# Cross-attention values in one 512-column product, and two heads' weighted sums moved behind half an output product

## The chip, the cores and the metric

The kernel runs on one core of a Trainium2 chip. The metric is the device time of one execution in microseconds; smaller is better. It is one launch that holds the whole decoder trunk of two layers, with every weight streamed from HBM once.

## The reference, cut to what matters

Each of the two layers has three token mixers that run side by side, a cross-attention into 256 memory tokens, and a SwiGLU FFN. The change touches the cross-attention and the last FFN product of the second layer.

```python
def cross_attention(h, mm, wq, wk, wv, wo):
    q = (h @ wq).reshape(B, S, XA_HEADS, XA_HEAD_DIM)     # S = 256 tokens, 4 heads of 256
    k = (mm @ wk).reshape(B, M, XA_HEADS, XA_HEAD_DIM)    # M = 256 memory tokens
    v = (mm @ wv).reshape(B, M, XA_HEADS, XA_HEAD_DIM)
    s = jnp.einsum('bshd,bmhd->bhsm', q, k).astype(jnp.float32) * (XA_HEAD_DIM ** -0.5)
    p = jax.nn.softmax(s, axis=-1).astype(v.dtype)
    o = jnp.einsum('bhsm,bmhd->bshd', p, v).reshape(B, S, D_MODEL)   # D_MODEL = 1024
    return o @ wo
...
x = x + (jax.nn.silu(h @ w1[l]) * (h @ w3[l])) @ w2[l]    # D_FF = 2816
```

## The kernel before, in words

**Split products.** Every float32 matrix is kept as two parts, `hi` (rounded to the format fp32r that TensorE takes) and `lo` (what is left), and a product is hi·hi + hi·lo + lo·hi. So a weight tile is made ready in three steps. `fetch` (lines 93 to 110) asks for a tile `raw` of 128 x 1024 by a DMA from SP's queue (line 102), ScalarE (ACT) rounds it into `hi` (line 106), and VectorE (DVE) subtracts to get `lo` (line 107, recorded as line 67, the helper `tt`). There are 5 buffers of `raw` and 4 each of `hi` and `lo`. Tile n therefore takes the `hi` and `lo` buffers of tile n-4, and its rounding waits until TensorE has read the last of tile n-4. `weights(cols)` hands out the next columns of this one stream, so the order of the stream in HBM is the order of the matmuls. `plan` (lines 79 to 87) says from which columns each tile is filled; the first 8 tiles of a layer are gathered from two runs, in pieces of 512 columns.

**Orders.** TensorE's instructions run in the order in which the code issues them (`InOrder`, line 43 in every row of TensorE). On ACT, DVE, GpSimd (POOL) and SP a scheduler sets the order of the instructions when the program is built, and each engine then works through its list in that order, waiting where an operand or a buffer is not there yet.

**The stage around the change.** After queries and keys, the values are made by `chunk_N`: activations are stationary, and a weight row of `n` columns moves, three matmuls for each of 2 blocks of memory tokens and each of 8 steps k. `values` (lines 538 to 541) calls it three times: columns 0 to 511 as one product with n = 512, then 512 to 767 and 768 to 1023 as two products with n = 256. Each result lies in PSUM as `xv` and is evicted into the tile `vt`: ACT writes the hi part (line 540), DVE the lo part (line 541, recorded as line 67). Between the steps, hooks issue the scores (`s`), the transposes of the softmax (`pT`, `turned`) and the weighted sums (`av`, `weighted`). `weighted(h)` is 12 matmuls of 256 columns for head h. It reads `vt` in the order block 0 hi (2 matmuls), block 0 lo (1), block 1 hi (2), block 1 lo (1), for two halves of the head's columns. Its result is split into `ox` by ACT and DVE. Heads 0 and 1 lie in the columns 0 to 511 of `vt`, heads 2 and 3 in 512 to 1023.

The output product `xo` (`chunk_T`) comes in chunks of 256 output columns. The first two chunks are cut in half: their steps k = 0 to 3, which read heads 0 and 1 of `ox`, come first, and k = 4 to 7 later. Before, the order is weighted(2), half of chunk 0, weighted(3), half of chunk 1:

```python
for c in range(2):
    weighted(2 + c)
    xo[c] = chunk_T(of(ox), KT, f"xo{l}_{c}", ks=range(0, 4))
```

A half chunk is 16 matmuls and uses exactly one weight tile. In layer 1 the second half of the values takes tiles 82 to 85, the half of chunk 0 tile 86, and the half of chunk 1 tile 87.

**The end of the program.** The last FFN product has three chunks of 256 columns (`chunk_T`) and two of 128 (`chunk_y` with one block, names w2_6 and w2_7), 22 steps each. Then the final norm follows.

Of the kernel before, what the change touches and what calls it, by code (L numbers as in the profile page):

```python
# [11 lines left out]
F32 = mybir.dt.float32  # L12
F32R = mybir.dt.float32r
AF = mybir.ActivationFunctionType
ALU = mybir.AluOpType
AX = mybir.AxisListType

P = 128
D = 1024
S = 256  # L20
L = 2
KT = D // P
FF = 2816
FT = FF // P
EPS = 1e-6
TW = 1024
LAYER_COLS = 163840
NPAR = 48
WARM = 9
AHEAD = 1  # L30

IN = dict(ax=0, ac=256, ab=512, q=768, k=1024, v=1280, g=1792, z=2304, gates=2816)


# [20 lines left out]
def decoder_trunk(ctx: ExitStack, tc: tile.TileContext, a, out):  # L55
    nc = tc.nc
    V, A, G, T = nc.vector, nc.scalar, nc.gpsimd, InOrder(tc, nc.tensor)
# [6 lines left out]
    pss = ctx.enter_context(tc.tile_pool(name="pss", bufs=4, space=bass.MemoryType.PSUM))  # L64

    def tt(e, o, x, y, op):
        e.tensor_tensor(o, x, y, op=op)  # L67

    def f32(t):
        return t.bitcast(F32)  # L70
# [5 lines left out]
    ws = a["ws"]  # L76
    tiles = ws.shape[0]

    pair_of = [(c + 512 * k, 512) for k in range(KT) for c in (0, 512 * KT)]
    plan = pair_of + [(c, TW) for c in range(2 * 512 * KT, LAYER_COLS, TW)]  # L80
    plan = [(l * LAYER_COLS + c, n) for l in range(L) for c, n in plan]
    pieces = []
    for c, n in plan:
        if not pieces or pieces[-1][-1][0] + pieces[-1][-1][2] == TW:
            pieces.append([])
        at = sum(m for _, _, m in pieces[-1])
# [25 lines left out]
    def weights(cols):  # L112
        pos = state["pos"]
        while state["loaded"] <= min(pos // TW + AHEAD, tiles - 1):
            fetch()
        o = pos % TW
        state["pos"] = pos + cols
        hi, lo = ready[pos // TW]
        return hi[:, o:o + cols], lo[:, o:o + cols]


    def chunk_T(xs, kt, name, hooks=None, ps=None, ks=None):


        if ps is None:
            ps = psm.tile([P, 2, 2, S], F32, tag="mm", name=name)
        for k in ks or range(kt):
            if hooks and k in hooks:
                hooks[k]()
            wh, wl = weights(2 * P)  # L130
            x = xs(k)
            for i in range(2):
                c = slice(i * P, (i + 1) * P)
                T.matmul(ps[:, i].rearrange("p t s -> p (t s)"), wh[:, c], x.rearrange("p t s -> p (t s)"),
                         start=(k == 0), stop=False, skip_group_check=True)
                T.matmul(ps[:, i, 1], wl[:, c], x[:, 0], start=False, stop=(k == kt - 1), skip_group_check=True)
        return ps

    def chunk_N(xs, name, hooks=None, n=512):

        ps = psm.tile([P, 2, 512], F32, tag="mm", name=name)
        for k in range(KT):
            if hooks and k in hooks:
                hooks[k]()
            wh, wl = weights(n)
            x = xs(k)
            for b in range(2):
                sl = slice(b * P, (b + 1) * P)
                T.matmul(ps[:, b, 0:n], x[:, 0, sl], wh, start=(k == 0), stop=False)
                T.matmul(ps[:, b, 0:n], x[:, 1, sl], wh, start=False, stop=False)  # L150
                T.matmul(ps[:, b, 0:n], x[:, 0, sl], wl, start=False, stop=(k == KT - 1))
        return ps[:, :, 0:n]

    def chunk_pair(xs, names, hooks):

        pair = [psm.tile([P, 2, 512], F32, tag="mm", name=name) for name in names]
        for k in range(KT):
            if k in hooks:
                hooks[k]()
            x = xs(k)  # L160
            for ps in pair:
                wh, wl = weights(512)
                for b in range(2):
                    sl = slice(b * P, (b + 1) * P)
                    T.matmul(ps[:, b], x[:, 0, sl], wh, start=(k == 0), stop=False)
                    T.matmul(ps[:, b], x[:, 1, sl], wh, start=False, stop=False)
                    T.matmul(ps[:, b], x[:, 0, sl], wl, start=False, stop=(k == KT - 1))
        return pair

    def chunk_y(xs, kt, name, n=2):  # L170

        ps = pss.tile([P, 2, S], F32, tag="sm", name=name)
        for k in range(kt):
            wh, wl = weights(n * P)
            x = xs(k)
            for i in range(n):
                c = slice(i * P, (i + 1) * P)
                T.matmul(ps[:, i], wh[:, c], x[:, 0], start=(k == 0 and i == 0), stop=False, skip_group_check=True)
                T.matmul(ps[:, i], wh[:, c], x[:, 1], start=False, stop=False, skip_group_check=True)
                T.matmul(ps[:, i], wl[:, c], x[:, 0], start=False, stop=(k == kt - 1 and i == n - 1),  # L180
                         skip_group_check=True)
        return ps

    def of(t, k0=0):
        return lambda k: t[:, k0 + k]
# [19 lines left out]
    xT = res.tile([P, KT, S], F32, name="xT")  # L205
    xs = res.tile([P, KT, 2, S], F32R, name="xs")
# [99 lines left out]
    for l in range(L):  # L306
# [5 lines left out]
        def pair(x):  # L312
            return x.rearrange("p b (h d) -> p b h d", h=8)
# [15 lines left out]
        t, ra, rbb = pair(mb[:, 0:2]), pair(mb[:, 2:4]), pair(mb[:, 4:6])  # L329
# [47 lines left out]
        for h in range(4):  # L377
            ps = pss.tile([P, 512], F32, tag="sm", name=f"sc{l}_{h}")
# [12 lines left out]
        for g in range(4):  # L391
            sl = slice(g * 64, (g + 1) * 64)
# [20 lines left out]
        for b in range(2):  # L413
            ps = pss.tile([P, 512], F32, tag="sm", name=f"o{l}_{b}")
# [27 lines left out]
        for c in range(12):  # L442
            t = summed(chunk_T(of(xs), KT, f"gt{l}_{c}"))
# [10 lines left out]
            if c == 6:  # L454
                if l == 0:
                    rows_kept(rm_n, "rm", rm)
                mmt = wrk.tile([P, KT, 2, S], F32R, tag="M", name=f"mmt{l}", bufs=1)
# [7 lines left out]
            if c == 1:  # L465
                for i in range(2):
                    ps = transposes(rr.rearrange("p b h d -> p b (h d)"), 2 * i, f"rT{l}")
                    for j in range(2):
                        f = 2 * i + j
# [4 lines left out]
        for c in range(4):  # L474
            ev = []
            for br, (k0, kn) in enumerate(((0, 2), (2, 4), (6, 2))):
                ps = chunk_y(of(mo, k0), kn, f"y{l}_{c}_{br}")
# [32 lines left out]
        vt = wrk.tile([P, 2, 2, D], F32R, tag="B", name=f"vt{l}", bufs=1)  # L510
# [24 lines left out]
        def turned(h):  # L535
            split(pt[:, 2 * h:2 * h + 2], transposes(pps[h], 0, f"pT{l}_{h}"))

        def values(c, n, hooks):
            ps = chunk_N(of(mmt), f"xv{l}_{c}", hooks, n)
            A.activation(vt[:, :, 0, c:c + n], ps, AF.Copy)  # L540
            tt(V, vt[:, :, 1, c:c + n], ps, f32(vt[:, :, 0, c:c + n]), ALU.subtract)

        ox = wrk.tile([P, 8, 2, S], F32R, tag="op", name=f"ox{l}", bufs=2)

        def weighted(h):
            ps = pss.tile([P, 2, S], F32, tag="sm", name=f"av{l}_{h}")
            for d in range(2):
                ns = slice((2 * h + d) * P, (2 * h + d + 1) * P)
                for b in range(2):
                    m = 2 * h + b  # L550
                    T.matmul(ps[:, d], vt[:, b, 0, ns], pt[:, m, 0], start=(b == 0), stop=False)
                    T.matmul(ps[:, d], vt[:, b, 0, ns], pt[:, m, 1], start=False, stop=False)
                    T.matmul(ps[:, d], vt[:, b, 1, ns], pt[:, m, 0], start=False, stop=(b == 1))
            split(ox[:, 2 * h:2 * h + 2], ps)

        def at(**kw):
            fs = dict(s=scores, t=turned, w=weighted)
            return {int(k[1:]): (lambda f=fs[v[0]], h=int(v[1]): f(h)) for k, v in kw.items()}

        qhooks = [None, None, at(k4="s0"), at(k4="s1", k6="t0")]  # L560
        for j in range(4):
            split(qx[:, 2 * j:2 * j + 2], summed(chunk_T(of(xs), KT, f"q{l}_{j}", hooks=qhooks[j])))
        values(0, 512, at(k1="s2", k2="t1", k4="s3", k6="t2"))
        values(512, 256, at(k2="t3", k6="w0"))
        values(768, 256, at(k4="w1"))


        xo = [None, None]
        for c in range(2):
            weighted(2 + c)  # L570
            xo[c] = chunk_T(of(ox), KT, f"xo{l}_{c}", ks=range(0, 4))

        acc = new_acc(f"acc_ffn{l}")
        for j in range(4):
            if j < 2:
                ps = chunk_T(of(ox), KT, f"xo{l}_{j}", ps=xo[j], ks=range(4, KT))
            else:
                ps = chunk_T(of(ox), KT, f"xo{l}_{j}")
# [22 lines left out]
        hooks = {2: {0: ffn_cols}, 3: {0: ffn_rows}}  # L601
        ts = []
        part = [chunk_T(of(xs), KT, f"f{l}_{c}", ks=range(0, KT - 2)) for c in range(2)]
        for c in range(FT):
            if c < 2:
                ps = chunk_T(of(xs), KT, f"f{l}_{c}", ps=part[c], ks=range(KT - 2, KT))
            else:
                ps = chunk_T(of(xs), KT, f"f{l}_{c}", hooks=hooks.get(c))
# [18 lines left out]
    table = wrk.tile([P, 1], F32, tag="table", name="table", bufs=1)  # L627
    A.activation(table, acc[:, 0:1], AF.Sqrt)
    for n in (6, 7):
        ps = chunk_y(hidden, FT, f"w2_{n}", 1)  # L630
        tt(V, xT[:, n], ps[:, 0], xT[:, n], ALU.add)
        tt(V, lastsq[:, n - 6], xT[:, n], xT[:, n], ALU.mult)
        if n == 6:
            tt(G, acc, acc, lastsq[:, 0], ALU.add)
            for m in range(7):
                V.tensor_scalar_mul(xT[:, m], xT[:, m], gfin[:, m:m + 1])
# [33 lines left out]
def _stream(x, l):  # L670
    w = x["w_in"][l]
    c = lambda n, m: w[:, IN[n]:IN[n] + m]
    parts = [_rows(c(n, 512), 512) for n in ("q", "v", "z", "g")]
# [57 lines left out]
```

## Time and profile before

| what | value |
|---|---|
| median of 3 runs | 968.31 us (968.21, 968.31, 970.08) |
| profiled execution, its own time | 969.4 us |
| span of that execution, first to last instruction | 967.6 us |
| TensorE (PE) busy | 951.8 us, 98% of the span |
| VectorE (DVE) busy | 713.7 us, 74% |
| ScalarE (ACT) busy | 539.8 us, 56% |
| mean granted TensorE clock | 0.995 |

The span is what the profile's rows lie in; 1.8 us of the execution's own time lie around it. A row of a timeline gives the start and the length of an instruction (of a run of alike ones, with their count), and in brackets the idle time of its engine ahead of it and what ended that. The ends of matmuls are modelled, so the pace of TensorE is read from start to start. A granted clock of 1.00 is TensorE's upper level (2.4 GHz), 0.50 its lower one (1.2 GHz).

### The profile page before, as it was taken

What the parts mean: (1) busy time and instruction counts of PE and PEld (TensorE: products, weight loads), DVE (VectorE), ACT (ScalarE), POOL (GpSimd) and SP (SyncE); (2) the same over time, 40 slices, a digit from 0 to 9 for tenths busy, and PEclk for the clock granted to TensorE, in tenths of its full rate; (3) what the DMA queues carried; (4) which work ended last, traced back from release to release, by engine and by line L of the source; (5) the groups of instructions that cost most, each with busy time, mean ns of one, the idle gap of its engine ahead of it and who ended that gap; (6) DMA issues with size and microseconds to landing.
All of it is one profiled execution on the core that took longest, in us unless ns stands there. A gap on an engine that the chain in (4) does not pass through costs nothing.

```text
span 967.6 us, 14606 instructions
## 1 busy us (share of the span) xinstructions
PE 951.8 (98%) x5622; PEld 836.8 (86%) x5622; DVE 713.7 (74%) x884; ACT 539.8 (56%) x740; POOL 296.1 (31%) x232
## 2 busy tenths in 40 slices
PE   8999999999999999999999989999999999999996
PEld 6788889888998888888888878998889888888886
DVE  7679789886768866657655896799776778666654
ACT  6565765565645755654456465545665466656431
POOL 5943021320114644432134230024100345444211
PEclk9999999999999999999999999999999999999998
DMA  9664665555546565555656355555644556556541
GB/s 310 245 228 145 192 203 186 190 182 170 172 133 194 177 198 191 193 187 180 197 179 194 111 180 193 195 179 172 196 153 151 154 187 191 187 194 194 180 151 44
DMA packets 52630, 175.53 MB, mean 181 GB/s; under 512 B 6096, under 2 KB 6608, under 8 KB 52560
## 3 DMA queue, kind: packets, MB, share of 16 engines
q1 hardware_dynamic: 52128, 174.03, 55.9%
q8 instruction: 44, 0.72, 0.3%
q10 hardware_dynamic: 432, 0.57, 0.2%
q14 instruction: 26, 0.21, 0.1%
HBM read 173.53 MB, written 1.05 MB: 180 GB/s over the span
## 4 chain that ended last, share of the span: by engine, by line
PE 96%; DVE 2%; DMA 1%; issue 0%; SPq 0%; ACT 0%; DVEq 0%
PE f L43 25%; PE gt L43 14%; PE w L43 13%; PE y L43 5%; PE k L43 5%; PE xo L43 5%; PE wo L43 5%; PE xv L43 5%; PE q L43 5%; PE z L43 2%; PE g L43 2%; PE v L43 2%; PE qk L43 2%; PE av L43 1%; PE ac L43 1%; PE s L43 1%
## 5 line engine op out<-in xcount | busy, mean ns | idle before, releaser
L67 DVE TENSOR_TENSOR lo<-raw,hi 128x1024 fp32r<-128x1024 f32 (+1 forms) x321 | 436.8, 1363 | 200.0 <-ACT hi L106 198.0
L106 ACT ACTIVATE hi<-raw 128x1024 fp32r<-128x1024 f32 (+1 forms) x321 | 338.9, 1057 | 315.1 <-issue 67.5
L43 PE MATMUL f<-xs,hi 128*128 128x512 f32 x704 | 245.2, 393 | 0.0
L43 PE MATMUL f<-xs,lo 128*128 128x256 f32 x704 | 196.1, 279 | 0.0
L43 PEld LDWEIGHTS f<-xs,hi 128*128 128x128 f32 x704 | 131.9, 187 | 30.1 <-issue 0.4
L43 PE MATMUL gt<-xs,hi 128*128 128x512 f32 x384 | 136.5, 400 | 2.8 <-DVE ev L67 2.7
L43 PEld LDWEIGHTS f<-xs,lo 128*128 128x128 f32 x704 | 132.6, 188 | 0.0
L67 POOL TENSOR_TENSOR sq<-xT 128x512 f32<-128x512 f32 x27 | 45.8, 1695 | 239.3 <-DVE xT L67 234.5
L43 PE MATMUL gt<-xs,lo 128*128 128x256 f32 x384 | 107.8, 281 | 0.0
L67 POOL TENSOR_TENSOR ev<-ev,rb_ffn 128x512 f32<-128x512 f32 x44 | 63.8, 1453 | 108.3 <-DVE ev L67 85.3
L43 PEld LDWEIGHTS gt<-xs,hi 128*128 128x128 f32 x384 | 72.7, 189 | 20.6 <-DVE ev L67 4.0
L43 PEld LDWEIGHTS gt<-xs,lo 128*128 128x128 f32 x384 | 73.2, 191 | 0.0
L43 PE MATMUL w<-aB,hi 128*128 128x512 f32 (+1 forms) x198 | 62.7, 372 | 0.0
L43 PE MATMUL w<-aA,hi 128*128 128x512 f32 (+1 forms) x198 | 62.3, 371 | 0.0
L67 POOL TENSOR_TENSOR ev<-ev 128x256 f32<-128x256 f32 x44 | 50.5, 1151 | 20.1 <-ACT ev L597 20.1
L202 DVE SCALAR_TENSOR_TENSOR xs<-xT,par,xs 128x256 fp32r<-128x256 f32 x48 | 49.1, 1062 | 4.2 <-ACT xs L201 4.2
L43 PE MATMUL w<-aB,lo 128*128 128x256 f32 x176 | 49.5, 281 | 0.0
L43 PE MATMUL w<-aA,lo 128*128 128x256 f32 x176 | 49.4, 281 | 0.0
L43 PE MATMUL y<-mo,hi 128*128 128x256 f32 x256 | 46.1, 283 | 0.0
L43 PE MATMUL k<-mmt,hi 128*128 128x512 f32 x128 | 45.6, 400 | 0.0
L43 PE MATMUL q<-xs,hi 128*128 128x512 f32 x128 | 45.5, 398 | 0.0
L43 PE MATMUL xo<-ox,hi 128*128 128x512 f32 x128 | 45.4, 399 | 0.0
(251 smaller groups left out, 1779.9 us busy)
## 6 DMA issues: line engine op xcount, KB each, us to landing
raw<-in_ws SPq DMA_DIRECT2D x304, 512.0 KB, 3.5
raw<-in_ws SPq DMA_DIRECT2D x32, 256.0 KB, 4.0
m<-in_memT SPq DMA_DIRECT2D x12, 256.0 KB, 4.0
xT<-in_xT SPq DMA_DIRECT2D x4, 256.0 KB, 5.2
dec<-in_dec SPq DMA_DIRECT2D x1, 512.0 KB, 6.0
wm<-in_wsT SPq DMA_DIRECT2D x2, 256.0 KB, 4.8
out<-xT ACTq DMA_DIRECT2D x2, 256.0 KB, 2.3
sgg<-in_sgg SPq DMA_DIRECT2D x1, 256.0 KB, 5.1
```

Of the source, the lines that this page charges most:

```text
L43: ins = getattr(self.engine, name)(*args, **kwargs)
L67: e.tensor_tensor(o, x, y, op=op)
L106: A.activation(hi[:, sl], raw[:, sl], AF.Copy)
L202: V.scalar_tensor_tensor(lo, x, scale, f32(hi), ALU.mult, ALU.subtract)
```

## The change

1. The second half of the values becomes one product with n = 512. The weights in HBM stay as they are (two runs of 256-column rows), so `plan` gathers each of the four tiles from both runs, in four pieces of 256 columns: 4 DMAs of 128 KB for a tile where 1 of 512 KB was.
2. `values` evicts a product block by block: 2 ACT and 2 DVE instructions of 128x512 for each product of 512 columns. The first product had one of 128x1024 on each engine, and the two of 256 columns one of 128x512 each.
3. The hooks in the second half move: the last `pT` at k = 2, weighted(0) at k = 4, weighted(1) at k = 6 of 8.
4. weighted(2) and weighted(3) come together, behind the half of chunk 0 of the output product.
5. w2_6 at the end of the program uses a new function, `chunk_1`: for a step k one matmul of 512 columns and one of 256, where three of 256 were. DVE adds its two sums in two steps.

```diff
+XV = 79872
...
+    def side(c0, n):
+        return [(c0 + n * k + m, n) for k in range(KT) for m in (0, n * KT)]
+    xv = XV + 512 * KT
+    plan = side(0, 512) + [(c, TW) for c in range(2 * 512 * KT, xv, TW)]
+    plan += side(xv, 256) + [(c, TW) for c in range(xv + 512 * KT, LAYER_COLS, TW)]
...
+    def chunk_1(xs, kt, name):
+        ps = pss.tile([P, 2, S], F32, tag="sm", name=name)
+        for k in range(kt):
+            wh, wl = weights(P)
+            x = xs(k)
+            T.matmul(ps.rearrange("p t s -> p (t s)"), wh, x.rearrange("p t s -> p (t s)"),
+                     start=(k == 0), stop=False, skip_group_check=True)
+            T.matmul(ps[:, 1], wl, x[:, 0], start=False, stop=(k == kt - 1), skip_group_check=True)
+        return ps
...
-        def values(c, n, hooks):
-            ps = chunk_N(of(mmt), f"xv{l}_{c}", hooks, n)
-            A.activation(vt[:, :, 0, c:c + n], ps, AF.Copy)
-            tt(V, vt[:, :, 1, c:c + n], ps, f32(vt[:, :, 0, c:c + n]), ALU.subtract)
+        def values(c, hooks):
+            ps = chunk_N(of(mmt), f"xv{l}_{c}", hooks)
+            for b in range(2):
+                A.activation(vt[:, b, 0, c:c + 512], ps[:, b], AF.Copy)
+                tt(V, vt[:, b, 1, c:c + 512], ps[:, b], f32(vt[:, b, 0, c:c + 512]), ALU.subtract)
...
-        values(0, 512, at(k1="s2", k2="t1", k4="s3", k6="t2"))
-        values(512, 256, at(k2="t3", k6="w0"))
-        values(768, 256, at(k4="w1"))
+        values(0, at(k1="s2", k2="t1", k4="s3", k6="t2"))
+        values(512, at(k2="t3", k4="w0", k6="w1"))
...
-        for c in range(2):
-            weighted(2 + c)
-            xo[c] = chunk_T(of(ox), KT, f"xo{l}_{c}", ks=range(0, 4))
+        xo[0] = chunk_T(of(ox), KT, f"xo{l}_0", ks=range(0, 4))
+        weighted(2)
+        weighted(3)
+        xo[1] = chunk_T(of(ox), KT, f"xo{l}_1", ks=range(0, 4))
...
-        ps = chunk_y(hidden, FT, f"w2_{n}", 1)
+        ps = chunk_1(hidden, FT, f"w2_{n}") if n == 6 else chunk_y(hidden, FT, f"w2_{n}", 1)
+        if n == 6:
+            tt(V, xT[:, n], ps[:, 1], xT[:, n], ALU.add)
```

**What it moves on the engines.** Three places, all in layer 1 at the end of the values; layer 2 has the same order with tiles 242 to 251. In the names, `hi89` is tile 89, `av0_2` the weighted sum of head 2 in layer 1, `xv0_512` the values' product that begins at column 512; the number behind the last underscore counts buffers. What an instruction waits for stands in brackets.

ACT, from weighted(1) to weighted(3), before:

```order
L198 ACTIVATE ox0_2170<-av0_1_2675 128x2x256 [waits PE_49]
L106 ACTIVATE hi89_2800<-raw89_2799 128x1024 [waits DMAHW6_49,DVE_49,PE_49]
L540 ACTIVATE vt0_2169<-xv0_768_2644 128x2x256 [waits PE_49]
L198 ACTIVATE ox0_2170<-av0_2_2722 128x2x256 [waits PE_49]
L106 ACTIVATE hi90_2831<-raw90_2830 128x1024 [waits DMAHW0_49,DVE_49,PE_49]
L198 ACTIVATE ox0_2170<-av0_3_2760 128x2x256 [waits PE_49]
```

The same stretch of ACT now:

```order
L215 ACTIVATE ox0_2170<-av0_1_2650 128x2x256 [waits PE_49]
L112 ACTIVATE hi89_2765<-raw89_2764 128x1024 [waits DMAHW2_49,PE_49,Activation_49]
L558 ACTIVATE vt0_2169<-xv0_512_2564 128x512 [waits PE_49]
L112 ACTIVATE hi90_2796<-raw90_2795 128x1024 [waits DMAHW3_49,DVE_49,PE_49]
L558 ACTIVATE vt0_2169<-xv0_512_2564 128x512 [waits DVE_49]
L215 ACTIVATE ox0_2170<-av0_2_2710 128x2x256 [waits PE_49]
L215 ACTIVATE ox0_2170<-av0_3_2725 128x2x256 [waits PE_49]
```

The eviction of block 0 stands behind `hi89`, that of block 1 behind `hi90`, which writes the buffer of tile 86.

DVE, the same stretch, now:

```order
L68 TENSOR_TENSOR lo89_2766<-raw89_2764,hi89_2765 128x1024 [waits DVE_49,DMAHW2_49,PE_49,Activation_49]
L68 TENSOR_TENSOR vt0_2169<-xv0_512_2564,vt0_2169 128x512 [waits Activation_49]
L68 TENSOR_TENSOR lo90_2797<-raw90_2795,hi90_2796 128x1024 [waits DMAHW3_49,PE_49,Activation_49]
L68 TENSOR_TENSOR vt0_2169<-xv0_512_2564,vt0_2169 128x512 [waits Activation_49]
L68 TENSOR_TENSOR ox0_2170<-av0_2_2710,ox0_2170 128x2x256 [waits Activation_49]
```

Before, the eviction `vt` from `xv0_768` stood on DVE behind `lo89`, with `lo90` after it; now the lo part of block 1 stands behind `lo90`.

TensorE (PE), from the last matmuls of the half of chunk 0 (tile 86) to the half of chunk 1, now:

```order
L44 MATMUL xo0_0_2687<-ox0_2170,hi86_2666 128x512
L44 MATMUL xo0_0_2687<-ox0_2170,lo86_2667 128x256
L44 MATMUL av0_2_2710<-pt0_2168,vt0_2169 128x256 [waits Activation_49]
L44 MATMUL av0_2_2710<-pt0_2168,vt0_2169 128x256
L44 MATMUL av0_2_2710<-pt0_2168,vt0_2169 128x256 [waits DVE_49]
L44 MATMUL av0_2_2710<-pt0_2168,vt0_2169 128x256 [waits Activation_49]
L44 MATMUL av0_2_2710<-pt0_2168,vt0_2169 128x256
L44 MATMUL av0_2_2710<-pt0_2168,vt0_2169 128x256 [waits DVE_49]
L44 MATMUL av0_2_2710<-pt0_2168,vt0_2169 128x256 x6
L44 MATMUL av0_3_2725<-pt0_2168,vt0_2169 128x256 [waits PE_49]
L44 MATMUL av0_3_2725<-pt0_2168,vt0_2169 128x256 x11
```

Before, the weighted sum of head 2 stood ahead of the matmuls of tile 86 and waited for ACT and for DVE once each; now it stands behind them and waits four times, for each block's hi and lo part.

## Rows read from the trace of the kernel before

**Rows 1.** The page's part 1: busy time of TensorE, share of the span, instructions.

```profile
PE 951.8 (98%) x5622; PEld 836.8 (86%) x5622; DVE 713.7 (74%) x884; ACT 539.8 (56%) x740; POOL 296.1 (31%) x232
```

**Rows 2.** The page's part 4: the chain that ended last, by engine.

```profile
PE 96%; DVE 2%; DMA 1%; issue 0%; SPq 0%; ACT 0%; DVEq 0%
```

**Rows 3.** The chain in order of time, layer 1: start, us, what.

```profile
44.05 10.89 PE g L43 x48
...
268.39 2.88 PE xv L43 x24
271.27 1.44 PE av L43 x12
```

**Rows 4.** Timeline of TensorE, layer 1, second half of the values to weighted(3).

```profile
256.29 0.40 PE L43 MATMUL xv<-hi,mmt 128*128 128x256 f32 x2
...
272.55 0.40 PE L43 MATMUL xo<-ox,hi 128*128 128x512 f32 x1
...
275.38 1.60 PE L43 MATMUL av<-pt,vt 128*128 128x256 f32 x12
```

**Rows 5.** Timeline of ACT: tiles 82, 89, eviction, 90 (layer 1), 250 (layer 2).

```profile
246.16 1.04 ACT L106 ACTIVATE hi<-raw 128x1024 fp32r<-128x1024 f32 x1
...
271.19 1.06 ACT L106 ACTIVATE hi<-raw 128x1024 fp32r<-128x1024 f32 x1 [2.16 <-PE xv L43]
272.15 0.58 ACT L540 ACTIVATE vt<-xv 128x512 fp32r<-128x512 f32 x1
...
275.46 1.06 ACT L106 ACTIVATE hi<-raw 128x1024 fp32r<-128x1024 f32 x1 [2.11 <-PE xo L43]
...
751.55 1.06 ACT L106 ACTIVATE hi<-raw 128x1024 fp32r<-128x1024 f32 x1 [2.11 <-PE xo L43]
```

**Rows 6.** Timeline of DVE, layer 1: tile 77, tile 89, eviction of the values' last quarter.

```profile
231.26 1.23 DVE L67 TENSOR_TENSOR lo<-raw,hi 128x1024 fp32r<-128x1024 f32 x1 [1.01 <-ACT hi L106]
...
272.28 1.22 DVE L67 TENSOR_TENSOR lo<-raw,hi 128x1024 fp32r<-128x1024 f32 x1 [2.49 <-ACT hi L106]
273.42 0.68 DVE L67 TENSOR_TENSOR vt<-xv,vt 128x512 fp32r<-128x512 f32 x1
```

**Rows 7.** Stretches: length, busy PE, PEld, DVE, ACT, POOL; granted clock, DMA share, GB/s.

```profile
0.00:20.00 20.00, 16.04 (x66) 12.72 (x67) 14.50 (x16) 12.20 (x18) 13.25 (x18) 1.00 0.91 318
...
578.00:580.00 2.00, 2.00 (x10) 1.66 (x9) 2.00 (x4) 0.77 (x2) 0.00 (x0) 0.61 0.85 262
580.00:582.00 2.00, 2.00 (x8) 1.73 (x7) 1.30 (x3) 0.44 (x1) 0.00 (x0) 0.54 0.75 250
```

**Rows 8.** Timeline of TensorE, layer 2, gates: around its longest wait there.

```profile
574.80 0.28 PE L43 MATMUL gt<-xs,lo 128*128 128x256 f32 x1
577.19 0.50 PE L43 MATMUL gt<-xs,hi 128*128 128x512 f32 x1 [2.11 <-DVE ev L67]
...
578.36 0.55 PE L43 MATMUL gt<-xs,hi 128*128 128x512 f32 x1
...
582.01 0.40 PE L43 MATMUL gt<-xs,hi 128*128 128x512 f32 x1
```

**Rows 9.** Timeline of TensorE at the start of the program: its longest wait there.

```profile
6.13 0.73 PE L43 MATMUL qk<-hi,xs 128*128 128x512 f32 x2 [0.93 <-ACT hi L106]
```

**Rows 10.** Timeline of TensorE, last FFN product: 24 pairs, then 43 triples to the last one.

```profile
933.70 0.40 PE L43 MATMUL w<-aA,hi 128*128 128x512 f32 x1
...
942.17 0.40 PE L43 MATMUL w<-aA,hi 128*128 128x256 f32 x2
...
957.35 0.40 PE L43 MATMUL w<-aB,hi 128*128 128x256 f32 x2
```

**Rows 11.** Timeline of DVE at the end: the add behind w2_7.

```profile
957.91 0.42 DVE L67 TENSOR_TENSOR xT<-w,xT 128x256 f32<-128x256 f32 x1 [6.43 <-PE w L43]
```

**Rows 12.** The page's part 6: weight DMAs, count, KB each, median us from issue to landing.

```profile
raw<-in_ws SPq DMA_DIRECT2D x304, 512.0 KB, 3.5
raw<-in_ws SPq DMA_DIRECT2D x32, 256.0 KB, 4.0
```

More of the change, by code (lines that the diff above doesn't have):

```diff
@@ L77, in decoder_trunk @@
     tiles = ws.shape[0]
-    pair_of = [(c + 512 * k, 512) for k in range(KT) for c in (0, 512 * KT)]
-    plan = pair_of + [(c, TW) for c in range(2 * 512 * KT, LAYER_COLS, TW)]
+    def side(c0, n):
[3 more added lines that the diff above has]
+    plan += side(xv, 256) + [(c, TW) for c in range(xv + 512 * KT, LAYER_COLS, TW)]
     plan = [(l * LAYER_COLS + c, n) for l in range(L) for c, n in plan]
@@ L137, in chunk_T, with chunk_N @@
         return ps
-    def chunk_N(xs, name, hooks=None, n=512):
+    def chunk_N(xs, name, hooks=None):
         ps = psm.tile([P, 2, 512], F32, tag="mm", name=name)
@@ L144, in chunk_N @@
                 hooks[k]()
-            wh, wl = weights(n)
+            wh, wl = weights(512)
             x = xs(k)
@@ L148, in chunk_N @@
                 sl = slice(b * P, (b + 1) * P)
[L149 to L152, printed above, removed]
+                T.matmul(ps[:, b], x[:, 0, sl], wh, start=(k == 0), stop=False)
+                T.matmul(ps[:, b], x[:, 1, sl], wh, start=False, stop=False)
+                T.matmul(ps[:, b], x[:, 0, sl], wl, start=False, stop=(k == KT - 1))
+        return ps
     def chunk_pair(xs, names, hooks):
@@ L168, in chunk_pair @@
         return pair
+    def chunk_1(xs, kt, name):
[6 more added lines that the diff above has]
+            T.matmul(ps[:, 1], wl, x[:, 0], start=False, stop=(k == kt - 1), skip_group_check=True)
+        return ps
     def chunk_y(xs, kt, name, n=2):
```

## The prediction, made before the change was run

> **What bounds the kernel now.** I read the page first, then the chain, then the timelines of the three engines that hand work to each other at the end of the values. The page shows TensorE busy for 98% of the span [rows 1], and the chain that ended last runs through it for 96% [rows 2]. So a change is worth what it does to TensorE's own list: matmul time that goes is won in full, and each wait put into that list is lost in full. In the piece of the chain around the change, values, weighted sums and output product follow each other without another engine's name between them [rows 3]; there is no wait to win there, only matmul time.
>
> The timelines of ACT and DVE show the second thing. ACT rounds a weight tile as soon as TensorE has finished the tile whose buffer it takes: the rounding of tile 90 began at 275.46, when the half of chunk 0 (tile 86) had been followed on TensorE by weighted(3) at 275.38, thus 0.08 us later, and the wait ahead of it was for that product [rows 4, 5]. Layer 2 reads alike at 751.55 [rows 5]. Roundings are thus paced by TensorE, and what stands behind one in ACT's list is paced by it too.
>
> **The change part by part.**
>
> *One product of 512 columns.* A triple of 512-column matmuls (one step k, one block) takes 10.89 / 16 = 0.68 us, read from the product `g`, which has the same form; a triple of 256 columns takes 2.88 / 8 = 0.36 us [rows 3]. Of these 32 a layer go and 16 of the wide ones come: 32 x 0.36 - 16 x 0.68 = 11.52 - 10.88 = 0.64 us a layer saved, all of it on the path. The Trainium skill, "TensorE: Matmul & The Clock Gate", section "Back-to-back issue gap", has the gap at N / 2.4 + 2.5 ns, so that merging two matmuls would save one fixed 2.5 ns: an estimate by that page of 48 x 2.5 ns = 0.12 us a layer, and a sum that is 1.0 us higher over both layers than mine. The rows of this kernel have a dearer 256-column matmul, 120 ns against 227 / 2, so I keep 0.64.
>
> *The evictions and weighted(2).* I count from the start of the half of chunk 0, which is now the first work behind the values (t = 0).
> - The half takes 275.38 - 272.55 = 2.83 us [rows 4], so weighted(2) begins at t = 2.83. A matmul of it takes 1.44 / 12 = 0.12 us [rows 3]; its fourth, the first that reads block 1, would start at 3.19, its sixth, which reads block 1's lo part, at 3.43.
> - Block 0: `hi89` starts 0.08 after the values end, `vt` hi begins 272.15 - 271.19 = 0.96 later and takes 0.58 [rows 5]; on DVE the lo part begins 273.42 - 271.19 = 2.23 after `hi89` and takes 0.68 [rows 5, 6]. That is t = 2.99, and the third matmul wants it at 3.07. It just fits.
> - Block 1 stands behind `hi90` on ACT, and `hi90` takes the buffer of tile 86, which the half of chunk 0 reads. So `hi90` begins at 2.83 + 0.08 = 2.91, block 1's hi part at 3.87, and it ends at 4.45. On DVE `lo90` and then the lo part follow: 2.91 + 2.23 = 5.14, ending at 5.82.
> - TensorE therefore waits from 3.19 to about 4.49, does two matmuls, and waits again to about 5.86 for what it wanted at 3.43 (0.04 us for the hand-over is my estimate): 2.43 us. The first matmul behind a wait is longer, 0.50 against 0.40 us [rows 8], so I take 2.5 us a layer, with 2.4 and 2.7 as ends.
>
> Who waits on whom, in one line: TensorE for block 1, block 1 for the rounding of tile 90, that rounding for TensorE's own half chunk. Moving two weighted sums behind 2.83 us of matmuls was to cover the eviction, and half of the eviction is tied to the end of that cover.
>
> *What is late next.* The split of heads 2 and 3 into `ox` is wanted by k = 4 to 7 of chunk 0, behind the half of chunk 1: 2.83 us of cover for one 0.6 us ACT and one 0.68 us DVE step, with no rounding ahead of them. Nothing.
>
> *The first product's eviction* is cut the same way, block 1 behind the rounding of tile 86. The second half starts at 256.29 [rows 4], its first tile ends 4 triples later at 259.01, so block 1's lo part is there at 259.01 + 0.08 + 2.23 + 0.68 = 262.0; weighted(0)'s sixth matmul comes at 256.29 + 8 x 0.68 + 0.43 (transposes, estimate) + 0.60 = 262.8. Spare: 0.8 us. I cost it at nothing; without that spare it is a wait.
>
> *The loads.* 12 more DMAs a layer on SP, in 128 KB pieces. The request for tile 82 can go out once tile 77 is through DVE, at 231.26 + 1.23 = 232.5, and the tile is used at 246.16: 13.7 us ahead [rows 5, 6]. Tiles in halves landed in 4.0 us against 3.5 [rows 12]; 128 KB pieces do not occur, so between 3.5 and, if four halves' times simply followed each other, 16 us; I take the near end, as the pieces are in flight together, and nothing on the path. On SP one load of memory tokens for the next layer falls behind one weight tile; nobody needs it in this stage.
>
> *w2_6.* 24 pairs (512 + 256) took 942.17 - 933.70 = 8.47 us, 0.353 each; 43 triples of 256 took 957.35 - 942.17 = 15.18 us, 0.353 each [rows 10]. Equal, so 22 triples for 22 pairs save nothing. DVE's extra add, 0.42 us, fits in its 6.43 us of idle time behind w2_6 [rows 11].
>
> *Sum without the clock.* 2 x (2.5 - 0.64) = +3.7 us. On the profiled execution's 969.4 us that is 973.1; that execution is 1.1 us above the median, so from the median 968.31 + 3.7 = 972.0.
>
> *The clock.* In layer 2 TensorE stood still from its last start at 574.80 to 577.19, a wait of 2.11 us, and was then granted 0.61 and 0.54 of its clock, the lower level (1.2 GHz) for most of 578 to 582 [rows 7, 8]. There 6 pairs took 582.01 - 578.36 = 3.65 us, where 6 x 0.353 = 2.12 is usual: 1.5 us lost. A wait of 0.93 us at the start was followed by no fall, the stretch has 1.00 [rows 7, 9]. The new standstill is 2.4 us, cut in two by 0.24 us of work, so it lies at the first of these rows by its sum, and nearer the second by its pieces. I give each layer an even chance of losing 1.5 us: 0, 1.5 or 3.1 us, one fall being the likeliest. The three runs of before lie at 968.2, 968.3 and 970.1, which fits a fall that comes in some executions only. The Trainium skill, same page, table "Why this matters for your kernels", warns only of idle gaps longer than any wait forecast here; by that rule no fall would come and the time would be 972.0. The row of layer 2, a fall behind 2.11 us, speaks against it.
>
> Forecast: 968.31 + 3.7 + 1.5 = 973.5.
>
> **The rivals.**
> - *Not slower: the eviction gets by.* If block 1's eviction ran before the rounding of tile 90, or that rounding 2.43 us earlier (at about t = 0.48), nothing would wait, and 2 x 0.64 is left: 968.31 - 1.3 = 967.0, within 0.2%. For it: the cover of 2.83 us is longer than ACT and DVE need for two evictions, 2 x 0.58 and 2 x 0.68 [rows 5, 6]. Against: the order as built, and a rounding that in both layers began only when TensorE had left the tile [rows 5]. It decides from the point where `hi90` starts. Chance 0.11, of which 0.03 for a gain of more than 0.2%.
> - *No clock fall*: 972.0, chance 0.25. *Both layers fall*: 975.0, chance 0.18.
> - *weighted(0) waits too*: the 0.8 us of spare are used up, some 1 us a layer: 975.5, chance 0.05. For it: the split adds a step on each engine, and the roundings drift with DVE's load.
> - *The change is not free on the loads*: the four pieces of a tile come later than 13.7 us after the request; each us late is a us. Against: the slack. Around 976, chance 0.03.
>
> **How the numbers follow.** One fall 0.38, none 0.25, both 0.18, weighted(0) 0.05, loads 0.03, no wait 0.11. A measurement can tell about 0.2% from no change, 1.9 us. All cases but the last are slower by more: 0.89. The last gives 0.08 for the same and 0.03 for faster. The range leaves out the no-wait case and the far end: from 972.0 less the low end of the waits and a us of scatter, 971.0, to 976.0, both falls with the upper end of the waits.
>
> **What would show it right or wrong.** On TensorE's timeline: behind the half of chunk 0 three matmuls of `av`, a wait for ACT of about 1 us, two matmuls, a wait for DVE of about 1 us, in both layers. On ACT: `hi90` about 0.08 us behind the end of the half, then `vt`. The values' second half shorter by 0.6 us. w2_6 unchanged. The windows behind the waits at 1.00 or near 0.5 decide the last 3 us. If `av` runs without a gap there, the central step is wrong.

## The result, and the profile after

| what | before | changed |
|---|---|---|
| median of 11 runs each, on one chip | 969.5 us (968.21 to 972.3) | 976.38 us (973.04 to 978.24) |
| ratio changed / before, 95% interval | | 1.0066 (1.0052 to 1.008) |
| profiled execution, its own time | 969.4 us | 976.66 us |
| its span | 967.6 us | 974.9 us |
| mean granted TensorE clock | 0.995 | 0.993 |

The change makes the kernel slower: 0.66% of 969.5 us is 6.4 us, with 5.0 to 7.8 us as the interval (the medians themselves lie 6.9 us apart). The forecast was 5.2 us, to 973.5 us. On the median that the forecast started from, 968.31 us, the ratio gives 974.7 us, inside its range; the kernel before itself ran 1.2 us higher beside it than in its first three runs, which puts the changed median, 976.38 us, 0.4 us above the range's upper end. Executions in a slow state of the chip are left out of all ratios: one of 2421 us among the 12 of "Evictions ahead of the second rounding only", and one of 1336 us of the kernel before beside it.

The page's busy times and the chain by engine first, the changed kernel's rows against [rows 1, 2]:

```profile
PE 955.9 (98%) x5504; PEld 833.6 (86%) x5504; DVE 713.1 (73%) x887; ACT 539.7 (55%) x742; POOL 296.7 (30%) x232
...
PE 94%; DVE 3%; issue 1%; ACT 1%; DMA 0%; DVEq 0%
```

There are 118 matmuls fewer and TensorE is busy for 4.1 us longer: a busy time that grows while work goes is a slower clock or a slower pace, not work. And the chain has passed 2% of its length from TensorE to ACT, DVE and the issue between them. TensorE's own list of waits names the place; columns are the waiting product, what it waits for, us in total, times, and the longest:

```profile
PE gt L44 <- DVE ev L68: 2.5, 3, 2.1
PE av L44 <- ACT vt L558: 2.2, 2, 1.1
PE av L44 <- DVE vt L68: 1.7, 2, 0.9
```

The first was there before [rows 8]. The two others are new: the weighted sums `av` wait for the eviction `vt`, once a layer for ACT and once for DVE. The timeline of TensorE in layer 1, for the stretch of [rows 4]:

```profile
257.09 0.62 PE L44 MATMUL xv<-hi,mmt 128*128 128x512 f32 x2
...
271.37 0.39 PE L44 MATMUL xo<-ox,hi 128*128 128x512 f32 x1
...
274.18 0.57 PE L44 MATMUL av<-pt,vt 128*128 128x256 f32 x3
275.85 0.50 PE L44 MATMUL av<-pt,vt 128*128 128x256 f32 x2 [1.10 <-ACT vt L558]
277.23 3.89 PE L44 MATMUL av<-pt,vt 128*128 128x256 f32 x19 [0.88 <-DVE vt L68]
280.92 0.59 PE L44 MATMUL xo<-ox,hi 128*128 128x512 f32 x1
```

Three matmuls, a wait for ACT, two matmuls, a wait for DVE, as forecast. What ACT and DVE did in that stretch, to be read beside [rows 5, 6]:

```profile
271.39 1.06 ACT L112 ACTIVATE hi<-raw 128x1024 fp32r<-128x1024 f32 x1 [1.97 <-PE xv L44]
272.35 0.58 ACT L558 ACTIVATE vt<-xv 128x512 fp32r<-128x512 f32 x1
274.26 1.06 ACT L112 ACTIVATE hi<-raw 128x1024 fp32r<-128x1024 f32 x1 [1.33 <-PE xo L44]
275.22 0.58 ACT L558 ACTIVATE vt<-xv 128x512 fp32r<-128x512 f32 x1
...
272.48 1.23 DVE L68 TENSOR_TENSOR lo<-raw,hi 128x1024 fp32r<-128x1024 f32 x1 [2.34 <-ACT hi L112]
273.62 0.69 DVE L68 TENSOR_TENSOR vt<-xv,vt 128x512 fp32r<-128x512 f32 x1
275.35 1.23 DVE L68 TENSOR_TENSOR lo<-raw,hi 128x1024 fp32r<-128x1024 f32 x1 [1.04 <-ACT hi L112]
276.49 0.69 DVE L68 TENSOR_TENSOR vt<-xv,vt 128x512 fp32r<-128x512 f32 x1
```

ACT stood idle for 1.33 us ahead of `hi90` at 274.26 with block 1's eviction queued behind it; the rounding was released by `xo`, the half chunk that was to cover the eviction. In layer 2 the chain of waits itself runs through the same five steps (start, us, what):

```profile
751.94 2.71 PE xo L44 x15
...
754.67 1.07 ACT hi L112
...
755.76 1.22 DVE lo L68
756.99 0.61 DVE vt L68
...
757.64 2.54 PE av L44 x19
```

Half chunk, rounding, its lo part, the eviction's lo part, weighted sums: TensorE waits for something that waits for TensorE. The last row is 2.54 us long and its twin in layer 1 is 3.89 us. The stretches show why (columns as in [rows 7], the granted clock is the third number from the end):

```profile
8.00:10.00 2.00, 2.00 (x7) 1.57 (x6) 0.95 (x1) 1.90 (x4) 1.30 (x2) 0.57 1.02 358
...
278.00:280.00 2.00, 2.00 (x11) 2.00 (x11) 0.69 (x1) 0.60 (x1) 0.00 (x0) 0.50 0.60 221
280.00:282.00 2.00, 2.00 (x11) 1.86 (x10) 0.21 (x1) 0.60 (x1) 0.00 (x0) 0.67 0.00 0
...
758.00:760.00 2.00, 2.00 (x19) 2.00 (x18) 0.59 (x1) 0.60 (x1) 0.00 (x0) 1.00 0.75 262
```

Behind the wait of layer 1 the clock fell to its lower level (1.2 GHz); behind that of layer 2 it stayed at 1.00. (The first of these stretches is another fall, near the start of the program, which comes back below.)

**Where the 7.3 us between the two spans lie.** From the start of the values' second half to the end of the weighted sums, layer 1 took 276.82 - 256.29 = 20.53 us before (276.82 is weighted(3)'s start in [rows 4] and its 1.44 us) and takes 280.92 - 257.09 = 23.83 us now: +3.3. Layer 2 gives +2.0 in the same way. So 5.3 us lie in the two stages of the change. The other 2.0 us lie in a stage that the change doesn't touch, the FFN's first product of layer 1, in the chain of waits of before and of the changed kernel:

```profile
314.41 105.39 PE f L43 x608
```

```profile
318.70 107.42 PE f L44 x608
```

In layer 2 both take 105.39 us. The rest nearly cancels: up to the second half's start in layer 1 it is 257.09 - 256.29 = 0.8 us longer, with a clock fall at 8 to 12 us in it (above), and in layer 2 no fall came behind the gates' wait of [rows 8] this time, so that the 256 matmuls there are 0.76 us shorter in the chain, before and now:

```profile
577.19 46.24 PE gt L43 x256
```

```profile
583.39 45.48 PE gt L44 x256
```

### The profile page after: what moved, and what is told of

Read it like the earlier page. It is cut to its first block, busy times and chain, and to the rows that moved or that the text cites. A ratio compares the mean times of both kernels' runs of the same rounds, so it can differ in the third digit from the quotient of the medians.

```text
span 974.9 us, 14439 instructions
## 1 busy us (share of the span) xinstructions
PE 955.9 (98%) x5504; PEld 833.6 (86%) x5504; DVE 713.1 (73%) x887; ACT 539.7 (55%) x742; POOL 296.7 (30%) x232
## 4 chain that ended last, share of the span: by engine, by line
PE 94%; DVE 3%; issue 1%; ACT 1%; DMA 0%; DVEq 0%
PE f L44 25%; PE gt L44 13%; PE w L44 13%; PE y L44 5%; PE k L44 5%; PE wo L44 5%; PE q L44 5%; PE xv L44 5%; PE xo L44 3%; PE z L44 2%; PE g L44 2%; PE v L44 2%; PE qk L44 2%; DVE lo L68 1%; PE av L44 1%; PE ab L44 1%
## 5 line engine op out<-in xcount | busy, mean ns | idle before, releaser
L44 PE MATMUL y<-mo,hi 128*128 128x256 f32 x256 | 46.2, 283 | 0.0
L44 PE MATMUL k<-mmt,hi 128*128 128x512 f32 x128 | 45.5, 399 | 0.0
L44 PE MATMUL wo<-mg,hi 128*128 128x512 f32 x128 | 45.3, 399 | 0.0
```

The source lines that it names most:

```text
L44: ins = getattr(self.engine, name)(*args, **kwargs)
```

## The experiments

In every run below the kernel before ran on the same chip, in turn with it, and ratios are to it; the chip is not the same for all runs, so runs are compared with each other by their ratios. The 24 matmuls of weighted(2) and weighted(3) stand in one piece in most of these kernels; I call them the block, and its length is from its first start to the start of what follows.

### Evictions ahead of both roundings

```diff
+    def behind(ins, first):
+        tc.add_manual_dep(...)
...
+            if held and n >= held[0]:
+                behind(ia, held[1])
+                behind(iv, held[2])
...
+            if c:
+                held[:] = [state["pos"] // TW + 3, ia, iv]
```

`ia` and `iv` are the ACT and DVE instruction of a rounding or of an eviction; from tile 89 (249 in layer 2) on, each rounding is put behind the last eviction of the second product in the order of its engine.

> The changed kernel with one more edit: on ACT and on DVE the two evictions of the values' second product are put ahead of the rounding of tile 89, and so ahead of that of tile 90. Theory (block 1's eviction waits for TensorE's own half chunk): block 1's hi part ends about 1.1 us after the values, its lo part about 2.0, both ahead of weighted(2) at 2.8; no wait of TensorE for vt in either layer, no fall of the clock there, and a time 1.3 us (2 x 0.64) below the kernel before, that is 4 to 8 us below the changed kernel. Rival (the loads in 128 KB pieces, or the merged product, cost the time): the waits may go, but the time stays 3 us or more above the kernel before.

Measured: 970.12 us (12 runs) against 971.21, ratio 0.9985 (0.9974 to 0.9996). Timelines of TensorE and ACT:

```profile
273.79 3.04 PE L44 MATMUL av<-pt,vt 128*128 128x256 f32 x24
276.67 0.40 PE L44 MATMUL xo<-ox,hi 128*128 128x512 f32 x1
...
271.18 0.60 ACT L568 ACTIVATE vt<-xv 128x512 fp32r<-128x512 f32 x1 [2.15 <-PE xv L44]
272.53 0.60 ACT L568 ACTIVATE vt<-xv 128x512 fp32r<-128x512 f32 x1 [0.76 <-DVE vt L569]
273.03 2.00 ACT L119 ACTIVATE hi<-raw 128x1024 fp32r<-128x1024 f32 x2
```

The block runs without a gap, 2.88 us to the next start in both layers, and no stretch of the output product behind it has a lower clock. What is left is the saving. As the instructions ran, each engine's list differs from the changed kernel's in nothing but the order of two evictions and two roundings on ACT and on DVE, once a layer, and the loss is gone: the rest of the change costs nothing that can be told. This version lies below both kernels, by 1.5 us against before (0.4 to 2.5), though its centre is below the 0.2% that one measurement tells from no change.

### Evictions ahead of the second rounding only

```diff
-                held[:] = [state["pos"] // TW + 3, ia, iv]
+                held[:] = [state["pos"] // TW + 4, ia, iv]
```

(against the version above: `hi89` stays ahead of the evictions, `hi90` goes behind them.)

> Edit: the changed kernel, with the evictions of the second values product ordered ahead of the rounding of tile 90 (and all later ones) on ACT and DVE, but still behind that of tile 89. Theory (the wait is the time by which an eviction in the list comes later than the matmul that reads it): from the end of the values, hi89 runs 0.08 to 1.1, block 0 hi to 1.6, lo89 on DVE to 2.3, block 0 lo to 3.0; block 1 hi on ACT follows DVE's block 0, to about 3.6 (wanted at 3.2), block 1 lo to about 4.3 (wanted at 3.4). TensorE waits some 0.9 to 1.0 us a layer instead of 2.0 to 2.4, so 2 x (1.0 - 0.64) = +0.7 us against the kernel before, ratio 1.0007, about 0.5% under the changed kernel, and no clock fall behind the half chunk. Rival (any standstill of TensorE there brings the fall and the full price): ratio 1.004 to 1.007 as the changed kernel.

Measured: 971.23 us (12 runs) against 970.41, ratio 1.0011 (0.9996 to 1.0025). TensorE, and ACT's eviction of block 1:

```profile
274.13 0.57 PE L44 MATMUL av<-pt,vt 128*128 128x256 f32 x3
274.95 0.50 PE L44 MATMUL av<-pt,vt 128*128 128x256 f32 x2 [0.24 <-ACT vt L568]
275.68 2.54 PE L44 MATMUL av<-pt,vt 128*128 128x256 f32 x19 [0.22 <-DVE vt L569]
...
274.30 0.60 ACT L568 ACTIVATE vt<-xv 128x512 fp32r<-128x512 f32 x1 [1.41 <-DVE vt L569]
```

The block takes 3.92 us, 1.04 more than without a wait, where 0.9 to 1.0 was expected; two such blocks less the saving of 0.54 us a layer make +1.0 us, and +1.1 us was measured (-0.4 to +2.4). The rival, that any standstill there brings the full price, falls. The last row shows what still holds block 1 on ACT: DVE's eviction of block 0, and not the rounding.

### weighted(2) back ahead of the half chunk

```diff
-        xo[0] = chunk_T(of(ox), KT, f"xo{l}_0", ks=range(0, 4))
         weighted(2)
+        xo[0] = chunk_T(of(ox), KT, f"xo{l}_0", ks=range(0, 4))
         weighted(3)
```

> Edit: the changed kernel, with weighted(2) put back ahead of the half of chunk 0, weighted(3) ahead of the half of chunk 1, as before the change; the merged product and the evictions by block stay. Theory (the move was not what costs; it hides part of what the eviction by blocks and its place in the lists cost): weighted(2) now wants block 1's lo part 0.6 us behind the values' end, and it comes, behind tile 89 and block 0's two steps, at about 4.3: a wait of about 3.7 us a layer, 2 x (3.7 - 0.64) = +6.1 us without the clock, and with falls behind standstills that long in both layers up to +9: ratio 1.006 to 1.009, at or above the changed kernel. Rival (the move of weighted(2) and (3) is the part that costs): time of the kernel before or below, ratio 0.998 to 1.000.

Measured: 979.55 us (5 runs), ratio 1.0094 (1.0079 to 1.0109), that is +9.1 us. TensorE in layer 1, and the chain in layer 2:

```profile
273.12 0.50 PE L44 MATMUL av<-pt,vt 128*128 128x256 f32 x2 [1.46 <-ACT vt L558]
274.49 0.48 PE L44 MATMUL av<-pt,vt 128*128 128x256 f32 x1 [0.88 <-DVE vt L68]
275.12 2.59 PE L44 MATMUL av<-pt,vt 128*128 128x256 f32 x9 [0.15 <-ACT vt L558]
```

```profile
748.52 2.54 PE xv L44 x11
...
755.45 1.50 PE av L44 x7
```

In layer 2 the values end at 748.52 + 2.54 = 751.1; the sixth matmul of weighted(2) would come 0.6 us later and came at 755.45, 3.8 us late where 3.7 was expected. Both layers had a clock fall behind it. The ratio came out just above the 1.006 to 1.009 that was expected. The move is thus not what costs; it hides some 1.3 us a layer (3.8 - 2.54) of a delay that comes from cutting the eviction by blocks and putting it behind the roundings.

### The move alone

The kernel before, with weighted(2) and weighted(3) behind the half of chunk 0 and nothing else changed:

```diff
-        for c in range(2):
-            weighted(2 + c)
-            xo[c] = chunk_T(of(ox), KT, f"xo{l}_{c}", ks=range(0, 4))
+        xo[0] = chunk_T(of(ox), KT, f"xo{l}_0", ks=range(0, 4))
+        weighted(2)
+        weighted(3)
+        xo[1] = chunk_T(of(ox), KT, f"xo{l}_1", ks=range(0, 4))
```

> The kernel before with one edit alone: weighted(2) and weighted(3) together behind the half of chunk 0, the values' second half still as two products of 256 columns with one eviction each. The last eviction then stands on ACT and DVE behind the rounding of tile 89 and ahead of that of tile 90. Theory: the move by itself costs nothing, as the last eviction ends about 3.0 us after the values and is wanted at about 4.3 by weighted(3): no wait of TensorE for vt, time of the kernel before within 1 us. Rival (moving the weighted sums is what costs, by a late ox for the second halves of the chunks): 2 us or more above the kernel before.

Measured: 970.15 us (12 runs), ratio 1.0005 (0.9989 to 1.0021). The median lies 1.1 us below the 971.21 of before and the centre of the ratio 0.5 us above it: no difference that can be told. The block takes 2.88 us in both layers, without a wait; in layer 1:

```profile
274.61 3.04 PE L43 MATMUL av<-pt,vt 128*128 128x256 f32 x24
```

With the eviction whole and ahead of the second rounding, the same place for the weighted sums is free.

### The weights of the second half in one piece

```diff
-    plan += side(xv, 256) + [(c, TW) for c in range(xv + 512 * KT, LAYER_COLS, TW)]
+    plan += [(c, TW) for c in range(xv, LAYER_COLS, TW)]
```

with the second half stored as rows of 512 columns, so that each of its tiles comes by one DMA of 512 KB instead of four of 128 KB.

> The changed kernel, but with the second half of the values laid out in HBM in rows of 512 columns, so that its four weight tiles a layer come by one DMA of 512 KB each instead of four of 128 KB; everything else as changed. Theory (the wait for the eviction): the same two waits of about 1.1 and 0.9 us a layer and the time of the changed kernel within 1.5 us. Rival (the small DMAs cost the time): 3 us or more below the changed kernel.

Measured: 975.9 us (6 runs), ratio 1.005 (1.0036 to 1.0065), against 1.0066 (1.0052 to 1.008) with the pieces: no difference that these intervals tell. The waits are those of the changed kernel, 2.2 us for ACT and 1.7 us for DVE. The loads are not the cause. The page of the changed kernel adds that each small piece even landed sooner (a tile is whole only with its fourth):

```profile
raw<-in_ws SPq DMA_DIRECT2D x296, 512.0 KB, 3.5
raw<-in_ws SPq DMA_DIRECT2D x32, 256.0 KB, 3.8
raw<-in_ws SPq DMA_DIRECT2D x32, 128.0 KB, 2.4
```

### w2_6 as before

```diff
-        ps = chunk_1(hidden, FT, f"w2_{n}") if n == 6 else chunk_y(hidden, FT, f"w2_{n}", 1)
-        if n == 6:
-            tt(V, xT[:, n], ps[:, 1], xT[:, n], ALU.add)
+        ps = chunk_y(hidden, FT, f"w2_{n}", 1)
```

> Edit: the changed kernel with w2_6 at the end computed as before, by three matmuls of 256 columns a step in place of one of 512 and one of 256. Theory: 22 pairs and 22 triples cost the same (0.353 us each), so the time is that of the changed kernel, ratio to the kernel before 1.0045 to 1.007. Rival (the pairs run at the 0.3467 us that they have in long stretches, or the triples bring a clock fall back): 22 x 0.007 = 0.15 us, below what can be measured.

Measured: 974.56 us (6 runs), ratio 1.005 (1.0033 to 1.0067): no difference to the changed kernel that can be told. This profile also serves for something else: its two blocks have the same waits as the changed kernel's and no clock fall behind either, and both take 5.42 us, so the wait by itself is 5.42 - 2.88 = 2.54 us a layer. In layer 1:

```profile
274.11 0.57 PE L44 MATMUL av<-pt,vt 128*128 128x256 f32 x3
...
279.53 0.40 PE L44 MATMUL xo<-ox,hi 128*128 128x512 f32 x1
```

### The standstill filled

20 matmuls into the product's own buffer, whose result the next matmul overwrites, ahead of weighted(2), so that TensorE works where it stood:

```diff
+            for i in range(fill):
+                T.matmul(ps[:, 0], vt[:, 0, 0, 0:P], pt[:, 0, 0], start=True, stop=True)
...
-        weighted(2)
+        weighted(2, 20)
```

> The changed kernel with 20 matmuls of 256 columns more in each layer, between the half of chunk 0 and weighted(2); their result is overwritten. They take 20 x 0.12 = 2.4 us, the length of the wait they stand in, so TensorE is busy where it stood still. Theory (2.4 us a layer of wait, and on top of it a clock that falls behind the standstill in part of the executions): waits for vt below 0.3 us, no stretch of granted clock 0.5 behind the half chunk, and a time 0.5 to 3 us below the changed kernel, still 3.5 to 4.5 us above the kernel before. Rival (no clock falls there, the waits are all): the time of the changed kernel within 0.5 us. Rival (the waits cost nothing, something else does): 4 us above the changed kernel.

Measured: 975.6 us (10 runs), ratio 1.0045 (1.0031 to 1.0059).

```profile
274.84 5.60 PE L44 MATMUL av<-pt,vt 128*128 128x256 f32 x44
```

No wait, and no fall behind it in either layer, and the time stays within about 2 us of the changed kernel. The 20 matmuls take the 2.5 us that the wait took (5.44 us from the first start to the next product), so this shows that filling a standstill doesn't win it back. How much of the time the falls make, this run can't tell: the gap to the changed kernel is 2.0 us, that to the version with whole tiles, which has the same waits, 0.5 us, and both intervals are 1.4 us either way.

### Further profiles of the same programs

The changed kernel twice more, the version with the evictions first once more; nothing is edited.

> Edit: none, the changed kernel once more, for a second profile of the same program. Theory (clock falls behind the new wait, and the pace of the long product f, are drawn anew in each execution): the waits are the same two per layer (block 24 weighted matmuls 5.4 us without a fall, 6.3 to 6.9 with one), but the layers that have a fall need not be layer 1 alone as before; and the 608 matmuls of f take either 105.39 or 107.42 us in each layer, not necessarily 107.42 then 105.39 again. Rival (both are a property of the program): a fall in layer 1 alone, and f at 107.42 in layer 1 and 105.39 in layer 2.

> Edit: none, the changed kernel a third time. Expected as for the second profile: by the theory falls and pace may differ from both earlier profiles; by the rival they repeat (fall in layer 1 alone, f 107.42 and 105.39).

> Edit: none, the kernel with the evictions ordered ahead of the roundings, once more. Theory: no wait for vt and no fall behind the half chunk again (24 weighted matmuls in 2.88 us in both layers), f at either 105.39 or 107.42 in each layer. Rival (pace belongs to the program): f at 105.39 in both layers, as in its first profile.

Measured, one execution each: 974.82 and 975.05 us against 971.81, and 969.39 us. The chain's rows for the long product `f` in the second profile of the changed kernel, in its third, and in the second of the version with the evictions first:

```profile
317.01 107.42 PE f L44 x608
...
795.82 105.39 PE f L44 x608
```

```profile
318.42 105.39 PE f L44 x608
...
796.31 105.39 PE f L44 x608
```

```profile
314.05 107.42 PE f L44 x608
...
790.39 105.39 PE f L44 x608
```

The changed kernel's third profile has 105.39 where its first two have 107.42; the other version has 107.42 where its first profile had 105.39. So the program alone doesn't set the pace. The falls differ as well: none behind the waits of the second profile (blocks of 5.42 and 5.44 us), one in layer 1 of the third (6.92 and 5.43). The rival falls on both counts. Whether the change makes the slow pace likelier is another question, and no run settles it: it stands in 0 of 4 such stages of the two kernels without the 512-column product (before, the move alone) and in 7 of 20 of the others.

## Why the prediction was right, and where it was off

- **The saving.** Forecast 0.64 us a layer, measured 0.54: from the second half's start to the half chunk's start, before 272.55 - 256.29 - 1.44 = 14.82 us (weighted(2) taken off), after 271.37 - 257.09 = 14.28. The triple of 512 columns was priced at 0.68 from the product `g`; here four take 2.75 us, 0.6875 each. The Trainium skill's section "Back-to-back issue gap", in "TensorE: Matmul & The Clock Gate", has its formula for a matmul by itself, and the estimate by it was 0.12 us a layer; the measured 0.54 stands with the row, not with it.
- **The wait.** This is the step that decided, and every number of it holds within 0.05 us. Counted from the half chunk's start at 271.37: `hi90` at 2.89 (forecast 2.91), block 1's hi part done at 4.43 (4.45), its lo part at 5.81 (5.82), block 0's lo part at 2.94 (2.99) and wanted at 3.05. The wait is 2.54 us a layer where 2.5 was taken. That the order on ACT and DVE makes it is shown from four sides: ahead of both roundings the wait is 0, behind one 1.04, behind the second, with TensorE as its releaser, 2.54; and 3.8 without the half chunk as cover.
- **Sum without the clock.** 2 x (2.54 - 0.54) = +4.0 us, forecast +3.7.
- **The clock.** The forecast gave each layer an even chance of a fall of 1.5 us. Ten waits of this length are in five profiles (three of the changed kernel, whole tiles, w2_6 as before); behind four of them the clock fell, behind none of the ten blocks without a wait or with the short one (evictions first, twice; behind one rounding; the move alone; the filled one). With a fall, the block and the rest of the output product behind it took 1.1 to 1.5 us longer. That makes about +1 us on average, an estimate from ten draws, beside the 1.5 us of the forecast. The row from which the forecast took its 1.5 us a fall, the gates of layer 2, is worth less over the whole stage: with a fall the 256 matmuls took 46.24 us before, without one 45.48 us in the changed kernel, because those behind the fall ran at the faster pace (some 0.347 us a pair against 0.353). Over all profiles they take 46.2 to 47.0 us with a fall and 45.5 without. The table "Why this matters for your kernels" of the Trainium skill's "TensorE: Matmul & The Clock Gate" warns only of longer gaps than these; the four falls speak against it as a bound.
- **The size.** +4.0 and about +1 make +5 us; measured were 6.4 (5.0 to 7.8) with the changed kernel, 4.9 in the two runs that have its waits unaltered (3.5 to 6.3 and 3.2 to 6.5). So the forecast of +5.2 us was of the right size; that its single fall, one of three cases, came near the average is in part luck. The 976.66 us of the profiled execution stand 3.2 us above the 973.5: 2.0 of them are one slow stage `f`, of which the prediction knew nothing, and the kernel before, too, ran 1.2 us above the median that the forecast started from.
- **The wait at the start.** The step "a wait of 0.93 us at the start was followed by no fall" doesn't carry over: the changed kernel's first wait there was 1.01 us and its clock fell at 8 to 12 us. Over all twelve profiles that first wait was 1.0 to 1.4 us in the five that have an early fall and 0.8 to 0.9 us in the seven that have none. But in three of the seven (behind one rounding, w2_6 as before, the second profile of the changed kernel) the two matmuls behind the wait took 1.22 us, against 0.73 in the other nine, and those behind them ran at half the pace until about 10 us, though the stretches there read 1.00; they can't show a fall. The wait ends at 6.0 to 6.3 us in all twelve and is longer where the 18 matmuls ahead of it end sooner (they took 3.65 to 4.08 us with a fall, 4.14 to 4.21 without), so wait and fall may have a cause in common. The change doesn't touch that stage, and none of this was tried.
- **What was costed at nothing.** weighted(0) didn't wait: block 1's lo part was done at 262.06 + 0.68 = 262.74 and wanted at 263.01 + 0.60 = 263.61, a spare of 0.87 us (forecast 0.8). The loads cost nothing, nor did the split of heads 2 and 3, nor w2_6: its 22 pairs take 957.15 - 949.41 = 7.74 us, 0.352 each, where 0.353 was forecast.
- **The rivals.** "Not slower" was worked out with its condition: if the eviction ran before the rounding of tile 90. Made true on the chip, it gives what it said, a saving and no wait. "weighted(0) waits" and "the loads" fell. Which of "no fall", one and two an execution gets is drawn anew each time: two of the five profiles above have none, two have one, and one has both.

What stays open: the exact part that clock falls have in the median (about +1 us by the ten waits; the filled run doesn't narrow it), whether the slow pace of `f` has a part in the 6.4 us beyond chance, and why ACT's eviction of block 1 waits for DVE's of block 0.

## What to carry to other kernels

When a consumer is moved behind other work to give its producer time, follow the producer's own queue: if ahead of it stands an instruction that the covering work itself releases, the wait can end only some time after that work does, here 277.23 - 274.18 = 3.05 us later. The work that the rounding waits for doesn't count as cover for what is queued behind it; only what comes after it does, as the 20 filling matmuls show, which left no wait but won nothing. Whether useful work there, such as the half of chunk 1, would have served was not run. Where an engine takes its list in order, as ACT and DVE do here, what the next product needs belongs ahead of what fills a buffer for a later one; that order alone took the 2.54 us to 0. And before two profiles are compared stage by stage, see whether a long stage that neither edit touches has another pace: here that is 2 us of the 7.3 between the two profiles.

## What the runs showed of the hardware

- **Two paces of TensorE at the full clock.** The 608 matmuls of `f` (pairs of 512 and 256 columns) take 105.39 or 107.42 us, 0.3467 or 0.3534 us a pair, and nothing between, in 24 stages of 12 profiles: 17 at the first, 7 at the second, with a granted clock of 1.00 in either. One program shows both, and one execution both in its two layers. What chooses the pace stays open.
- **Falls of the clock are not decided by the program alone.** The same wait of 1.10 and 0.88 us with two matmuls between was followed by the lower level in 4 of 10 cases, and the wait of 2.1 to 2.3 us in layer 2's gates in 8 of 12 profiles.
- **Small pieces.** DMAs of 128 KB, four to a tile, landed in a median of 2.4 us against 3.5 us for one of 512 KB, in this kernel's load.
